# A hybrid attention and retention encoder layer: its prelude loaded in eight transfers on two queues, x scaled before it is turned, and larger loads in phase 1

## The chip, the cores and the metric

The kernel runs on one core of a Trainium2 chip. The metric is device time in microseconds (us) of one execution. Three runs of the kernel before took 971.65, 972.60 and 973.26 us, median 972.6 us.

## The reference, cut to what matters

x has 512 rows of 2048 columns, all f32. A vector `c` gives a shift and a scale for each column of x, and a gate for each column of the output:

```
c_act = silu(c)
shift, scale, gate = split(c_act @ w_ada + b_ada, 3)        # w_ada 2048 x 6144
h = x * rsqrt(mean(x*x over a row) + eps) * g * (1 + scale) + shift   # norm, then modulation
proj = h @ w_in                                             # 2048 x 7168
q, k, v, z of 8 attention heads and 4 retention heads = split(proj)
y = concat(attention(...) * silu(z_a), retention(...) * silu(z_r))
out = rms_norm(x + gate * (y @ w_out), final_gain)
```

(`g` multiplies the normed x before the modulation; the kernel puts it into the scale.) No product with `w_in` can start before some 128 columns of h are there, and these need the norm of whole rows of x, and `c_act @ w_ada` for those columns.

## The kernel before, in words

**Exact products from three passes.** Every large operand is split into a high part (float32r) and the rest. A product is three matmuls: high by high (line 85), and the two mixed ones (line 87). ScalarE writes the high part of a piece of w_in (`whi`, line 543), VectorE the rest (`wlo`, line 544). A matmul with 512 moving columns follows the one before it by 0.23 us when nothing is waited for.

**The columns of h are made tile by tile.** The 2048 columns are 16 "k-tiles" of 128. Phase 1 multiplies the first 13 units of `w_in` (256 columns each) with them in chunks of 1, 2, 2, 3, 4 and 4 k-tiles (`CHUNKS`), while the modulation of the next chunk is being made. One k-tile costs phase 1 78 matmuls of 512 moving columns (13 units, two 128-column halves or their like, three passes). Sums over chunks are kept in SBUF (`acc`, line 941, VectorE), except for two units that keep their PSUM banks.

**The modulation of a chunk** (`ada_pieces`, line 188): blocks of `w_ada` are loaded into `araw`, three buffers of 4 KB a partition; VectorE multiplies each by its entry of silu(c) and adds it to `aacc` (line 216; the first one is ScalarE's, line 212); TensorE sums over the partitions; then shift, scale, `hh` (high part, ScalarE, line 168) and `hl` (the rest, VectorE, line 181). The steps lie in an agenda that is spread over the items that are fed; a step adds the block loaded three steps earlier and then issues the next load.

**The feed** (`feed`): an item is half a load of `w_in` (512 columns' worth). It is loaded, four items later (`LEAD`) split, two items later (`LOOK`) multiplied. Loads of `w_in` go into `raw`, three buffers of 4 KB a partition.

**The prelude** makes all this possible. SyncE's queue issues everything in this order: eight loads of the first tile's columns of `w_ada` (line 110, 256 KB each, 512-byte runs), among them the small rows of `c`, `b_ada` and the gain (lines 115, 118, 119), then x in eight half tiles of 512 KB (line 127), then `w_in` and `w_ada` for phase 1. VectorE multiplies and adds the 16 blocks of `w_ada` (lines 279, 281); TensorE needs only four short products to sum them (`sums0`, line 288). For each of the four tiles of 128 rows of x, ScalarE makes the sums of squares of both halves (line 302), VectorE and GpSimd the row factor (lines 308, 315, 319). TensorE turns the unscaled x 128 columns at a time (`turned`, line 343), or turns and scales it by a product with a diagonal matrix (`turned_scaled`, `k0_part`, lines 351, 377); where it was turned unscaled, VectorE multiplies the result by factors that were spread over all partitions (lines 331, 335, 373). `WARM` products of constants (lines 392, 396) keep TensorE at work early on.

**What sets the order.** An engine executes its instructions in one order, which a scheduler chose and which pinned instructions (`pin`) fix. A transfer issued from SyncE or ScalarE is counted by one of eight completion semaphores, taken in turn by both queues together; the ninth transfer waits until the first has landed, and that wait stands in the issuing engine's own queue.

Of the kernel before, what the change touches and what calls it, by code (L numbers as in the profile page):

```python
# [17 lines left out]
P = 128  # L18
# [33 lines left out]
def trunk_kernel(ctx, tc, x, c, norm_gain, w_ada, b_ada, w_in, w_out, dec_f, dec_b, final_gain, out):  # L52
# [36 lines left out]
    # ---------------- loads of c, of the first tile's columns of w_ada, of x  # L89
# [4 lines left out]
    # x transposed lies where the low part of h comes to lie, a tile for each chunk of k  # L94
# [49 lines left out]
    nc.scalar.activation(ce, ps0[:, 0:NK], AF.Exp, scale=-1.0)
# [7 lines left out]
    # an engine keeps to the traced order of pinned instructions  # L152
# [11 lines left out]
    # ---------------- modulation of k-tiles k0..k0+nk, then their h  # L164
# [23 lines left out]
    def ada_pieces(k0, nk):  # L188
        n = nk * P
        acc = aap.tile([P, 2, 4 * P], F32, tag="aacc", name="aacc")  # L190
        npc = max(1, 1024 // (2 * n))
# [3 lines left out]
        def load(kr):  # L195
            raw = aap.tile([P, 1024], F32, tag="araw", name="araw", bufs=AR)
            rv = raw[:, : npc * 2 * n].rearrange("p (a b f) -> p a b f", a=npc, b=2)
            src = wa[kr * P : (kr + npc) * P, 0 : 2 * D].rearrange(
                "(a p) (b f) -> p a b f", p=P, b=2
            )[:, :, :, k0 * P : k0 * P + n]  # L200
            if npc == 1:
                nc.sync.dma_start(rv[:, 0], src[:, 0])
            else:
                for b in range(2):
                    nc.sync.dma_start(rv[:, :, b], src[:, :, b])
            raws[kr] = rv
# [66 lines left out]
    nc.vector.tensor_copy(bg, ps0[:, 64:112])
    nc.vector.tensor_scalar_add(bg[:, 16:32], bg[:, 16:32], 1.0)
    acc0 = [aap.tile([P, 2 * P], F32, tag="acc0", name="acc0") for _ in range(2)]
    for k in range(NK):
        rv, c1 = raw0[k // 4][:, k % 4], ct[:, k : k + 1]
        if k < 2:
            nc.vector.tensor_scalar_mul(acc0[k], rv, c1)
        else:  # L280
            nc.vector.scalar_tensor_tensor(acc0[k % 2], rv, c1, acc0[k % 2], op0=ALU.mult, op1=ALU.add)
    rsb = aap.tile([P, S], F32, name="rsb", bufs=1)

    def sums0():
        psa = bank(psA, "psa")
        for i in range(2):
            for b in range(2):
                nc.tensor.matmul(
                    psa[:, b : b + 1], acc0[i][:, b * P : (b + 1) * P], ones[:, 0:1],
                    start=i + b == 0, stop=i == 1, skip_group_check=True,  # L290
                )
        return psa

    def shift_scale0(psa):
        nc.vector.tensor_tensor(sv[:, 0:1], psa[:, 0:1], bg[:, 0:1], op=ALU.add)
        nc.vector.tensor_tensor(av[:, 0:1], psa[:, 1:2], bg[:, NK : NK + 1], op=ALU.add)
        nc.vector.tensor_tensor(av[:, 0:1], av[:, 0:1], bg[:, 32:33], op=ALU.mult)

    def squares(t, h):
        sq = xp.tile([P, 1024], F32, tag="sq", name="sq")  # L300
        v = xn[t][:, h * 1024 : (h + 1) * 1024]
        marks["sq"] = pin(nc.scalar.activation(sq, v, AF.Square, accum_out=ssx[:, t, h : h + 1]))

    mss = {}

    def half_root(t):
        ms = mss[t] = small.tile([P, 2], F32, tag="ms2", name="ms2", bufs=2)
        pin(nc.vector.tensor_scalar(ms[:, 0:1], ssx[:, t, 0:1], 1.0 / D, EPS, op0=ALU.mult, op1=ALU.add))

    def roots(t):  # L310
        if t not in mss:
            half_root(t)
        ms = mss[t]
        pin(
            nc.vector.scalar_tensor_tensor(
                ms[:, 1:2], ssx[:, t, 1:2], 1.0 / D, ms[:, 0:1], op0=ALU.mult, op1=ALU.add
            )
        )
        nc.gpsimd.tensor_tensor(rsx[:, t : t + 1], ms[:, 1:2], mhalf[:, 0:1], op=ALU.pow)

    # the rows' factors: on a diagonal, then on every partition
    dgs = {}
    psbs = {}

    def diagonal(t):
        dg = dgs[t] = xp.tile([P, P], F32, tag="dg", name="dg", bufs=2)
        marks["dg"] = pin(nc.vector.tensor_scalar_mul(dg, ident, rsx[:, t : t + 1]))

    def spread(t):
        psb = bank(psA, "psb")[:, 0:P]  # L330
        pin(nc.tensor.matmul(psb, ones, dgs[t], start=True, stop=True))
        psbs[t] = psb

    def spread_out(t):
        pin(nc.vector.tensor_copy(rsb[:, t * P : (t + 1) * P], psbs[t]))
# [3 lines left out]
    def turned(t, b):  # L339
# [6 lines left out]
    def turned_scaled(t, b):  # L346
        ps = psx[t, b] = bank(psP, "psx")
        for j in range(4):
            k = 4 * b + j
            pin(  # L350
                nc.tensor.matmul(
                    ps[:, j * P : (j + 1) * P], xn[t][:, k * P : (k + 1) * P], dgs[t], start=True, stop=True
                )
            )

    def pieces(b):
        for i, g in enumerate(groups):
            lo, hi = max(g[0], 4 * b), min(g[-1] + 1, 4 * b + 4)
            if i and lo < hi:
                yield i, g, lo, hi  # L360

    def evacuated(t, b):
        for i, g, lo, hi in pieces(b):
            dst = xt_tiles[i][:, lo - g[0] : hi - g[0], t * P : (t + 1) * P]
            src = psx[t, b][:, (lo - 4 * b) * P : (hi - 4 * b) * P].rearrange("p (k f) -> p k f", k=hi - lo)
            pin(nc.scalar.copy(dst, src))

    def scaled(t, b):
        rt = rsb[:, t * P : (t + 1) * P].rearrange("p (a f) -> p a f", a=1)
        for i, g, lo, hi in pieces(b):  # L370
            dst = xt_tiles[i][:, lo - g[0] : hi - g[0], t * P : (t + 1) * P]
            src = psx[t, b][:, (lo - 4 * b) * P : (hi - 4 * b) * P].rearrange("p (k f) -> p k f", k=hi - lo)
            pin(nc.vector.tensor_tensor(dst, src, rt.to_broadcast([P, hi - lo, P]), op=ALU.mult))

    def k0_part(t):
        o = psk3[:, 0:P] if t == 3 else psk[:, t * P : (t + 1) * P]
        pin(nc.tensor.matmul(o, xn[t][:, 0:P], dgs[t], start=True, stop=True))

# [3 lines left out]
    # the first tile's h, its columns in two parts  # L382
# [8 lines left out]
    for _ in range(WARM):  # L391
        pin(nc.tensor.matmul(ps0[:, 128:256], ones, ident, start=True, stop=True))
    turned(0, 0)
    turned(0, 1)
    for _ in range(WARM2):
        pin(nc.tensor.matmul(ps0[:, 128:256], ones, ident, start=True, stop=True))
# [910 lines left out]
```

## Time and profile before

| what | value |
|---|---|
| times of three runs | 971.65, 972.60, 973.26 us (median 972.6) |
| profiled execution: its span, first to last instruction | 971.6 us (1.0 us under the median; no other time is given for it) |
| TensorE busy | 941.5 us, 97% of the span |
| VectorE busy | 618.0 us, 64% |
| ScalarE busy | 376.5 us, 39% |
| GpSimd busy | 10.6 us, 1% |
| read from HBM | 136.36 MB |
| share of the 16 DMA engines taken by SyncE's queue | 43.4% |

How to read it: times in views are microseconds from the first instruction. In the views PE is TensorE (PEld its weight loads), DVE is VectorE, ACT is ScalarE, POOL is GpSimd, SP is SyncE; SPq or ACTq is the engine's sequencer, which issues transfers. "idle before us <-releaser" in a row of groups, or the bracket in a row of the timeline, is how long the engine stood idle before it and what ended that. A row of windows gives, for each stretch, its length, busy time of PE, PEld, DVE, ACT and POOL with the number of instructions, the granted clock of TensorE as a share, the busy share of the 16 DMA engines and GB/s. A matmul in the program can be two instructions in the trace (f32 operands), and consecutive matmuls overlap.

### The profile page before, as it was taken

What the parts mean: (1) busy time and instruction counts of PE and PEld (TensorE: products, weight loads), DVE (VectorE), ACT (ScalarE), POOL (GpSimd) and SP (SyncE); (2) the same over time, 40 slices, a digit from 0 to 9 for tenths busy, and PEclk for the clock granted to TensorE, in tenths of its full rate; (3) what the DMA queues carried; (4) which work ended last, traced back from release to release, by engine and by line L of the source; (5) the groups of instructions that cost most, each with busy time, mean ns of one, the idle gap of its engine ahead of it and who ended that gap; (6) DMA issues with size and microseconds to landing.
All of it is one profiled execution on the core that took longest, in us unless ns stands there. A gap on an engine that the chain in (4) does not pass through costs nothing.

```text
span 971.6 us, 14377 instructions
## 1 busy us (share of the span) xinstructions
PE 941.5 (97%) x5556; PEld 820.4 (84%) x5556; DVE 618.0 (64%) x1101; ACT 376.5 (39%) x732; POOL 10.6 (1%) x22
## 2 busy tenths in 40 slices
PE   5989898999999999999999999999999999999996
PEld 4877687788988888988998899988899988888896
DVE  5879978977968786664555556745534382535444
ACT  3824242525235555444343232422333372333321
POOL 0000000000000000000000000000000000000001
PEclk9989999999999999999999999999999999999999
DMA  9786878763552222212224525425322148233304
GB/s 316 232 260 209 270 250 290 266 202 99 183 179 84 65 66 66 65 45 88 84 69 161 186 66 184 143 88 198 126 63 90 57 159 283 86 128 134 109 1 173
DMA packets 109715, 141.49 MB, mean 146 GB/s; under 512 B 6024, under 2 KB 78408, under 8 KB 109648
## 3 DMA queue, kind: packets, MB, share of 16 engines
q1 hardware_dynamic: 108496, 138.49, 43.4%
q10 hardware_dynamic: 1152, 2.10, 0.6%
q8 instruction: 43, 0.70, 0.3%
q14 instruction: 24, 0.20, 0.1%
HBM read 136.36 MB, written 4.20 MB: 145 GB/s over the span
## 4 chain that ended last, share of the span: by engine, by line
PE 89%; DMA 5%; DVE 3%; issue 2%; SPq 1%; ACT 0%; POOLq 0%; POOL 0%; DVEq 0%; ACTq 0%
PE pp L87 26%; PE pw L87 14%; PE pp L85 13%; PE po L87 12%; PE pw L85 7%; PE po L85 6%; PE op L87 3%; PE sp L87 2%; DMA raw<-in_w_in_dram 2%; DMA araw<-in_w_ada_dram 2%; PE op L85 2%; PE tp L770 1%; DVE aacc L216 1%; PE sp L85 1%; DMA xt<-in_x_dram 1%
## 5 line engine op out<-in xcount | busy, mean ns | idle before, releaser
L543 ACT CAST whi<-raw 128x512 fp32r<-128x512 f32 (+1 forms) x289 | 174.9, 606 | 435.8 <-PE pp L87 204.9
L544 DVE TENSOR_TENSOR wlo<-raw,whi 128x512 fp32r<-128x512 f32 (+1 forms) x289 | 193.9, 672 | 209.6 <-ACT whi L543 205.3
L85 PE MATMUL pp<-whi,hh 128*128 128x256 f32 x576 | 162.4, 282 | 0.0
L87 PE MATMUL pp<-wlo,hh 128*128 128x256 f32 x576 | 161.9, 281 | 0.0
L87 PE MATMUL pp<-whi,hl 128*128 128x256 f32 x576 | 161.5, 280 | 0.0
L85 PEld LDWEIGHTS pp<-whi,hh 128*128 128x128 f32 x576 | 108.5, 188 | 2.5 <-ACT sc L839 1.7
L87 PEld LDWEIGHTS pp<-wlo,hh 128*128 128x128 f32 x576 | 108.5, 188 | 1.0 <-DVE wlo L544 0.2
L87 PEld LDWEIGHTS pp<-whi,hl 128*128 128x128 f32 x576 | 108.5, 188 | 0.0
L85 PE MATMUL pw<-hh,whi 128*128 128x512 f32 x256 | 102.5, 401 | 3.6 <-DVE acc L941 3.6
L85 PE MATMUL pp<-hh,whi 128*128 128x512 f32 x256 | 102.7, 403 | 3.3 <-ACT hh L168 2.9
L87 PE MATMUL pp<-hh,wlo 128*128 128x512 f32 x256 | 102.1, 399 | 0.0
L87 PE MATMUL pp<-hl,whi 128*128 128x512 f32 x256 | 101.6, 397 | 0.0
L87 PE MATMUL pw<-hh,wlo 128*128 128x512 f32 x256 | 101.3, 396 | 0.0
L87 PE MATMUL pw<-hl,whi 128*128 128x512 f32 x256 | 101.1, 395 | 0.1
L87 PE MATMUL po<-wlo,yh 128*128 128x512 f32 (+1 forms) x252 | 92.6, 367 | 0.0
L85 PE MATMUL po<-whi,yh 128*128 128x512 f32 (+1 forms) x252 | 92.5, 367 | 0.0
L87 PE MATMUL po<-whi,yl 128*128 128x512 f32 (+1 forms) x252 | 92.5, 367 | 0.0
L216 DVE SCALAR_TENSOR_TENSOR aacc<-araw,ct,aacc 128x512 f32<-128x512 f32 (+2 forms) x75 | 76.1, 1014 | 10.8 <-DMA araw<-in_w_ada_dram 10.3
L941 DVE TENSOR_TENSOR acc<-acc,pw 128x512 f32<-128x512 f32 x100 | 66.3, 682 | 7.8 <-PE pw L87 7.3
L991 DVE SCALAR_TENSOR_TENSOR gacc<-graw,ct,gacc 128x512 f32<-128x512 f32 x60 | 45.0, 750 | 38.3 <-DMA graw<-in_w_ada_dram 38.0
L85 PEld LDWEIGHTS pp<-hh,whi 128*128 128x128 f32 x256 | 48.8, 191 | 16.7 <-ACT hh L168 3.0
L85 PEld LDWEIGHTS pw<-hh,whi 128*128 128x128 f32 x256 | 48.1, 188 | 17.3 <-DVE acc L941 5.7
(232 smaller groups left out, 1555.3 us busy)
## 6 DMA issues: line engine op xcount, KB each, us to landing
raw<-in_w_in_dram SPq DMA_DIRECT2D x94, 512.0 KB, 3.5
araw<-in_w_ada_dram SPq DMA_DIRECT2D x32, 512.0 KB, 5.5
graw<-in_w_ada_dram SPq DMA_DIRECT2D x64, 256.0 KB, 2.9
raw<-in_w_out_dram SPq DMA_DIRECT2D x32, 512.0 KB, 3.5
araw<-in_w_ada_dram SPq DMA_DIRECT2D x40, 256.0 KB, 3.7
raw<-in_w_in_dram SPq DMA_DIRECT2D x16, 384.0 KB, 5.4
araw<-in_w_ada_dram SPq DMA_DIRECT2D x16, 384.0 KB, 3.7
xt<-in_x_dram SPq DMA_DIRECT2D x8, 512.0 KB, 8.6
```

Source lines behind the costliest of these rows:

```text
L85: nc.tensor.matmul(o, lh, rh, start=start, stop=False, skip_group_check=True)
L87: nc.tensor.matmul(o, a, b, start=False, stop=stop and b is (rl if swap else rh), skip_group_check=True)
L216: ins = nc.vector.scalar_tensor_tensor(acc[:, :, :n], rv[:, a], ct[:, kr + a : kr + a + 1], acc[:, :, :n], op0=ALU.mult, op1=ALU.add,)
L543: c1 = nc.scalar.copy(dh, src)
L544: c2 = nc.vector.tensor_tensor(dl, src, f32(dh), op=ALU.subtract)
L770: nc.tensor.transpose(tp_[:, j * P : (j + 1) * P], pt[:, j * P : (j + 1) * P], ident)
L941: nc.vector.tensor_tensor(accs[u][i], accs[u][i], ps[i], op=ALU.add)
L991: nc.vector.scalar_tensor_tensor(st["acc"], raw, ct[:, kr : kr + 1], st["acc"], op0=ALU.mult, op1=ALU.add)
```

## The change

**Loads of the prelude.** The first tile's columns of `w_ada` come in four loads of 512 KB on SyncE's queue (two column blocks, `raw00` and `raw01`, shown as raw_105 and raw_106, in two halves of eight row blocks each). x comes in four loads of 1 MB on ScalarE's queue, a whole tile each. The rows of `c`, `b_ada` and the gain are issued by GpSimd, ahead of its constants. All loads of chunk 0's `w_in` are issued before anything of phase 1 is fed.

**The first tile's modulation.** VectorE's 16 multiplications and additions are gone. TensorE sums directly over rows with `w_ada` as the stationary operand and a column of silu(c) as the moving one: 32 products of one column (`sums0`), in four groups of eight, placed between the tiles of x.

**x.** Of a tile's squares ScalarE sums the left half (`squares_a`), VectorE the right half (a product that sums, with 1/D and eps in it). The factor then scales x in place before it is turned, on VectorE, in a 128-column piece, an 896-column piece, and later the right half. All turning is by the identity; results are copied out of PSUM by ScalarE (banks 0, 1, 3) and VectorE (bank 2). The diagonal, the spread factors and the products with them are gone. Products of constants stand in four places (`WARM = 8, 6, 5, 6`).

**Phase 1.** `araw` has 8 KB a partition, so that a step carries twice the row blocks of `w_ada`. Through the first four chunks every second load of `w_in` goes to one of three further buffers (`raw1`), and items are split eight items after they are loaded (`LEAD1`), from the fifth chunk on four as before. The last tile's results are copied out in four agenda steps from item 10 on.

```
-WARM = 9
-WARM2 = 1
-LATE_AT = 7, 8
+WARM = 8, 6, 5, 6
-RAW, WB, LOOK, LEAD, EB, YB = 3, 3, 2, 4, 1, 22
+RAW, RAW1, WB, LOOK, LEAD, LEAD1, EB, YB = 3, 3, 3, 2, 4, 8, 1, 22
...
     def raw_tile():
+        early["n"] += 1
+        if early["on"] and early["n"] % 2 == 0:
+            return aap.tile([P, 1024], F32, tag="raw1", name="raw1", bufs=RAW1)
         return wp.tile([P, 1024], F32, tag="raw", name="raw", bufs=RAW)
...
+    def load0(q, b, i):
+        q.dma_start(
+            raw0[b][:, i * 8 : (i + 1) * 8],
+            wa[i * 8 * P : (i + 1) * 8 * P, b * D : b * D + P].rearrange("(a p) f -> p a f", p=P),
+        )
+
+    for t in range(NT):
+        nc.scalar.dma_start(xn[t], x2[t * P : (t + 1) * P, :])
+    nc.gpsimd.dma_start(c_row, c.rearrange("b (k p) -> (b k) p", p=P))
+    for i in range(2):
+        for b in range(2):
+            load0(nc.sync, b, i)
+    nc.gpsimd.dma_start(bg_row[0:32, :], b_ada[:, 0 : 2 * D].rearrange("b (k p) -> (b k) p", p=P))
+    nc.gpsimd.dma_start(bg_row[32:48, :], norm_gain.rearrange("b (k p) -> (b k) p", p=P))
...
-        npc = max(1, 1024 // (2 * n))
+        npc = 2048 // (2 * n)
...
-            raw = aap.tile([P, 1024], F32, tag="araw", name="araw", bufs=AR)
+            raw = aap.tile([P, 2048], F32, tag="araw", name="araw", bufs=AR)
...
+    def sums0(b, i):
+        for a in range(8 * i, 8 * i + 8):
+            pin(
                 nc.tensor.matmul(
+                    psa[:, b : b + 1], raw0[b][:, a, :], ct[:, a : a + 1],
+                    start=a + b == 0, stop=a == NK - 1, skip_group_check=True,
                 )
+            )
...
+    warm(WARM[0])
+    squares_a(0)
+    squares(0)
+    silu_c()
+    for t in range(NT):
+        scaled(t, 0, P)
+        k0_part(t)
+        if t == 3:
+            break
+        scaled(t, P, 1024)
+        turned(t, 0)
+        turned(t, 1)
+        squares_a(t + 1)
+        squares(t + 1)
+        if t < 2:
+            warm(WARM[1 + t])
         if t == 0:
+            turn_rows()
+        else:
+            sums0(t - 1, 0)
+        evacuated(t, 0, act)
+        evacuated(t, 1, act)
+    for t in range(3):
+        scaled(t, 1024, D)
+        turned(t, 2)
+        turned(t, 3)
+        evacuated(t, 3, act)
+        if t:
+            evacuated(t - 1, 2, dve)
+    sums0(0, 1)
+    scaled(3, P, 1024)
+    evacuated(2, 2, dve)
+    marks["conv1"] = [marks[act], marks[dve]]
+    sums0(1, 1)
+    warm(WARM[3])
+    shift_scale0()
...
+        lead = LEAD1 if early["on"] else LEAD
+        while len(loaded) > (lead if item is not None else 0):
...
+        early["on"] = ci < len(CHUNKS) - 2
...
+        if ci == 0:
+            for it in items:
+                it["load"]()
```

ScalarE at the start of the program, before (sq is the junk result of the squares, xt_122 and xt_125 the first two tiles of x, psx a PSUM bank with turned x, DMAHW a completion semaphore of a transfer):

```order
L144 ACT_TABLE_LOAD
L144 ACTIVATE ce<-ps_145 128x16 [waits PE_49]
L302 ACTIVATE sq,ssx<-xt_122 128x1024 [waits DMAHW3_49]
L302 ACTIVATE sq,ssx<-xt_122 128x1024 [waits DMAHW4_49,Activation_49]
L302 ACTIVATE sq,ssx<-xt_125 128x1024 [waits DMAHW5_49,Activation_49]
L302 ACTIVATE sq,ssx<-xt_125 128x1024 [waits DMAHW6_49,Activation_49]
L366 COPY xT_96<-psx 128x4x128 [waits PE_49]
```

ScalarE at the start of the program, now (xt_107 to xt_110 are the four tiles of x):

```order
L121 DMA xt_107<-in_x_dram 128x2048
L121 DMA xt_108<-in_x_dram 128x2048
L121 DMA xt_109<-in_x_dram 128x2048
L121 DMA xt_110<-in_x_dram 128x2048 [waits DMAHW2_49]
L300 ACT_TABLE_LOAD
L300 ACTIVATE sqa,ssx<-xt_107 128x1024 [waits DMAHW0_49]
L272 ACTIVATE ce<-ps_143 128x16 [waits PE_49]
L300 ACTIVATE sqa,ssx<-xt_108 128x1024 [waits DMAHW3_49]
```

The four loads of x now stand ahead of all that ScalarE computes, and the fourth waits for semaphore 2; the rows after it, the table load and the first squares, stand behind that wait.

TensorE where the first tile's modulation is summed, before (acc_160 and acc_161 are VectorE's sums, dg the diagonal of row factors):

```order
L288 MATMUL psa<-ones,acc_160 128x1 [waits DVE_49]
L288 MATMUL psa<-ones,acc_160 128x1
L288 MATMUL psa<-ones,acc_161 128x1 [waits DVE_49]
L331 MATMUL psb<-dg,ones 128x128 [waits DVE_49]
L377 MATMUL psk<-dg,xt_122 128x128
L351 MATMUL psx<-dg,xt_122 128x128 x4
```

TensorE in the same part, now (raw_105 and raw_106 are the two column blocks of w_ada):

```order
L353 MATMUL ps_143<-ident,ones 128x128 x5
L286 MATMUL psa<-ct,raw_105 128x1 [waits DMAHW1_49]
L286 MATMUL psa<-ct,raw_105 128x1 x7
L322 MATMUL psk<-ident,xt_109 128x128 [waits DMAHW6_49,DVE_49]
L328 MATMUL psx<-ident,xt_109 128x128 [waits DVE_49,PE_49,Activation_49]
L328 MATMUL psx<-ident,xt_109 128x128 x2
L286 MATMUL psa<-ct,raw_106 128x1 [waits DMAHW2_49]
L286 MATMUL psa<-ct,raw_106 128x1 x7
L322 MATMUL psk_144<-ident,xt_110 128x128 [waits DMAHW2_49,DVE_49]
```

Four short products became 32, eight of them between two tiles of x, and the rows name semaphore 2 as that of SyncE's second load, the first half of raw_106.

TensorE just ahead of the first product with w_in, before:

```order
L351 MATMUL psx<-dg,xt_128 128x128 x8
L343 MATMUL psx<-ident,xt_131 128x128 x3
L377 MATMUL psk_307<-dg,xt_131 128x128
L343 MATMUL psx<-ident,xt_131 128x128 x4
L331 MATMUL psb<-dg,ones 128x128
L85 MATMUL pw<-hh_77,whi 128x512
```

TensorE just ahead of the first product with w_in, now:

```order
L328 MATMUL psx<-ident,xt_107 128x128 x8
L328 MATMUL psx<-ident,xt_108 128x128 x8
L328 MATMUL psx<-ident,xt_109 128x128 x8
L286 MATMUL psa<-ct,raw_105 128x1 x8
L286 MATMUL psa<-ct,raw_106 128x1 x8
L353 MATMUL ps_143<-ident,ones 128x128 x6
L328 MATMUL psx<-ident,xt_110 128x128 x7
L89 MATMUL pw<-hh_77,whi 128x512
```

The right halves of three tiles, half of the short products, six products of constants and seven turns of the last tile now stand in a row ahead of the first product.

More of the change, by code (lines that the diff above doesn't have):

```diff
@@ L200, in load @@
             )[:, :, :, k0 * P : k0 * P + n]
[L201 to L205, printed above, removed]
+            for b in range(2):
+                nc.sync.dma_start(rv[:, :, b], src[:, :, b])
             raws[kr] = rv
@@ L267, in ada_pieces @@
         )
-    nc.tensor.transpose(ps0[:, 64:112], bg_row, ident[0:48, 0:48])
     bg = const.tile([P, 48], F32, name="bg")
[L273 to L287, printed above, removed]
+    def turn_rows():
+        pin(nc.tensor.transpose(ps0[:, 64:112], bg_row, ident[0:48, 0:48]))
+        pin(nc.vector.tensor_copy(bg, ps0[:, 64:112]))
+        pin(nc.vector.tensor_scalar_add(bg[:, 16:32], bg[:, 16:32], 1.0))
+    def silu_c():
+        pin(nc.tensor.transpose(ps0[:, 0:NK], c_row, ident[0:NK, 0:NK]))
+        pin(nc.scalar.activation(ce, ps0[:, 0:NK], AF.Exp, scale=-1.0))
+        pin(nc.vector.tensor_scalar_add(ce, ce, 1.0))
+        pin(nc.vector.reciprocal(ce, ce))
+        pin(nc.vector.tensor_tensor(ct, ps0[:, 0:NK], ce, op=ALU.mult))
@@ L288, in sums0 @@
+    psa = bank(psA, "psa")
+    psk = bank(psA, "psk")
+    ps0 = bank(psA, "ps0")
+    psk3 = bank(psM, "psk3")
+    def sums0(b, i):
+        for a in range(8 * i, 8 * i + 8):
+            pin(
                 nc.tensor.matmul(
-                    psa[:, b : b + 1], acc0[i][:, b * P : (b + 1) * P], ones[:, 0:1],
-                    start=i + b == 0, stop=i == 1, skip_group_check=True,
-                )
[L292 to L297, printed above, removed]
@@ L314, in roots, with squares @@
+    def squares(t):
+        sd = aap.tile([P, 1024], F32, tag="aacc", name="sqd")
+        v = xn[t][:, 1024:2048]
+        pin(nc.vector.tensor_tensor_reduce(sd, v, v, 1.0 / D, EPS, ALU.mult, ALU.add, ssx[:, t, 1:2]))
+        ms = small.tile([P, 1], F32, tag="ms1", name="ms1", bufs=2)
         pin(
             nc.vector.scalar_tensor_tensor(
-                ms[:, 1:2], ssx[:, t, 1:2], 1.0 / D, ms[:, 0:1], op0=ALU.mult, op1=ALU.add
+                ms, ssx[:, t, 0:1], 1.0 / D, ssx[:, t, 1:2], op0=ALU.mult, op1=ALU.add
@@ L317, in roots @@
             )
         )
[L319 to L335, printed above, removed]
+        nc.gpsimd.tensor_tensor(rsx[:, t : t + 1], ms, mhalf[:, 0:1], op=ALU.pow)
@@ L337, in trunk_kernel, with scaled, k0_part, turned @@
+    def scaled(t, a, b):
+        v = xn[t][:, a:b]
+        marks["sc"] = pin(nc.vector.tensor_scalar_mul(v, v, rsx[:, t : t + 1]))
     psx = {}
-    def turned(t, b):
+    def k0_part(t):
+        o = psk3[:, 0:P] if t == 3 else psk[:, t * P : (t + 1) * P]
+        pin(nc.tensor.transpose(o, xn[t][:, 0:P], ident))
+    def turned(t, b, pin=pin):
         ps = psx[t, b] = bank(psP, "psx")
@@ L343, in turned, with evacuated @@
             pin(nc.tensor.transpose(ps[:, j * P : (j + 1) * P], xn[t][:, k * P : (k + 1) * P], ident))
[L346 to L356, printed above, removed]
+    def evacuated(t, b, eng):
         for i, g in enumerate(groups):
@@ L359, in pieces @@
             if i and lo < hi:
[L360 to L377, printed above, removed]
+                dst = xt_tiles[i][:, lo - g[0] : hi - g[0], t * P : (t + 1) * P]
+                src = psx[t, b][:, (lo - 4 * b) * P : (hi - 4 * b) * P].rearrange("p (k f) -> p k f", k=hi - lo)
+                marks[eng] = pin(eng(dst, src))
+    act, dve = nc.scalar.copy, nc.vector.tensor_copy
     hl[0] = hp.tile([P, 1, S], F32R, tag="g0", name="hl0")[:, 0, :]
@@ L389, in h0_low @@
         marks["hl"] = pin(nc.vector.tensor_tensor(hl[0][:, cols], tmp0[:, cols], f32(hh[0][:, cols]), op=ALU.subtract))
[L391 to L396, printed above, removed]
-    turned(0, 3)
-    for t in range(2):
-        squares(t, 0)
-        squares(t, 1)
-    roots(0)
-    psa = sums0()
@@ L403, in trunk_kernel @@
-    psk = bank(psA, "psk")
-    diagonal(0)
-    shift_scale0(psa)
-    spread(0)
-    k0_part(0)
-    spread_out(0)
-    for t in range(2):
-        turned_scaled(t, 2)
-        evacuated(t, 2)
-        squares(t + 2, 0)
-        squares(t + 2, 1)
-        scaled(t, 0)
-        turned(t + 1, 0)
-        half_root(t + 1)
-        scaled(t, 1)
-        turned(t + 1, 1)
-        roots(t + 1)
-        scaled(t, 3)
-        if t == 0:
-            turned(1, 3)
-        diagonal(t + 1)
-        if t == 1:
-            half_root(3)
-        spread(t + 1)
-        k0_part(t + 1)
-        spread_out(t + 1)
@@ L429, in trunk_kernel, with warm @@
-    marks["conv1"] = [marks["sq"]]
-    psk3 = bank(psM, "psk3")
-    turned_scaled(2, 2)
-    turned_scaled(2, 3)
-    roots(3)
-    scaled(2, 0)
-    turned(3, 0)
-    diagonal(3)
-    marks["conv1"].append(marks["dg"])
-    k0_part(3)
+    def warm(n):
+        for _ in range(n):
+            pin(nc.tensor.matmul(ps0[:, 128:256], ones, ident, start=True, stop=True))
+    warm(WARM[0])
[14 more added lines that the diff above has]
+            warm(WARM[1 + t])
+        if t == 0:
+            turn_rows()
[3 more added lines that the diff above has]
+        evacuated(t, 1, act)
@@ L446, in trunk_kernel @@
     h0_low(B)
-    spread(3)
-    turned(3, 2)
-    evacuated(2, 3)
-    turned(3, 3)
-    spread_out(3)
-    scaled(3, 0)
-    scaled(3, 1)
-    late = [lambda b=b: scaled(3, b) for b in (2, 3)]
+    scaled(3, 1024, D)
+    for b in range(4):
+        turned(3, b, lambda ins: ins)
+    late = [lambda b=b: evacuated(3, b, act if b % 2 else dve) for b in range(4)]
     x_scope.close()
@@ L889, in trunk_kernel @@
     fed = 0
-    for i, f in zip(LATE_AT, late):
-        agenda.setdefault(i, []).append(f)
+    for i, f in enumerate(late):
+        agenda.setdefault(LEAD1 + LOOK + i, []).append(f)
     def plan(fs, start, span):
```

59 lines of the change are left out of this document (15 added, 44 removed).

## The prediction

> **What bounds the kernel now.** I read the page's busy line, then windows, then the waits of the engine that fills them.
>
> ```profile
> span 971.6 us, 14377 instructions
> PE 941.5 (97%) x5556; PEld 820.4 (84%) x5556; DVE 618.0 (64%) x1101; ACT 376.5 (39%) x732; POOL 10.6 (1%) x22
> ```
>
> TensorE is the bound; only its 30 idle us and its slow clock can be won. The first product with w_in, then the windows after it:
>
> ```profile
> 28.75 0.50 PE L85 MATMUL pw<-hh,whi 128*128 128x512 f32 x1
> ```
>
> ```profile
> 28.00:40.00 12.00, 11.91 (x58) 9.18 (x58) 11.99 (x26) 10.62 (x22) 0.00 (x0) 1.00 0.58 181
> 40.00:50.00 10.00, 9.60 (x64) 8.39 (x62) 8.29 (x14) 6.21 (x13) 0.00 (x0) 1.00 0.87 272
> 50.00:60.00 10.00, 7.05 (x23) 5.71 (x23) 5.46 (x11) 2.98 (x5) 0.00 (x0) 0.66 0.82 259
> 60.00:110.00 50.00, 49.99 (x251) 41.52 (x250) 48.00 (x74) 16.95 (x34) 0.00 (x0) 1.00 0.73 235
> 110.00:170.00 60.00, 53.33 (x314) 45.33 (x313) 49.97 (x69) 19.62 (x42) 0.00 (x0) 1.00 0.80 272
> 170.00:220.00 50.00, 50.00 (x222) 39.92 (x223) 42.03 (x61) 20.30 (x53) 0.00 (x0) 1.00 0.69 228
> ```
>
> So the prelude costs 28.75 us, and phase 1 loses TensorE time at two places. In 50 to 60, 2.95 us are idle and the granted clock is 0.66: 10 x 0.34 = 3.4 us lost. In 110 to 170, 6.67 us are idle. With 0.5 ahead of 50 the losses are 13.5 us. After 170 TensorE has no gap, so a later first product carries to the end one for one. The waits behind the two places (the first row PE's from 28 to 240 us, the second VectorE's from 28 to 200: total, how often, longest), and the timeline at the first:
>
> ```profile
> PE pw L85 <- DVE acc L941: 4.7, 6, 1.7
> ```
>
> ```profile
> DVE aacc L216 <- DMA araw<-in_w_ada_dram: 8.7, 11, 3.2
> ```
>
> ```profile
> 49.18 1.05 PE L230 MATMUL psm<-ones,aacc 128*128 128x1 f32 x8 [0.40 <-DVE aacc L216]
> ...
> 51.80 0.62 ACT L543 CAST whi<-raw 128x512 fp32r<-128x512 f32 x1 [3.42 <-DMA raw<-in_w_in_dram]
> 52.32 1.51 ACT L168 ACTIVATE hh<-xT,sv,av 128x512 fp32r<-128x512 f32 x2
> 53.18 2.07 PE L85 MATMUL pp<-hh,whi 128*128 128x512 f32 x4 [2.95 <-ACT hh L168]
> ```
>
> At 50, `hh` of chunk 1 stood behind a split on ScalarE that waited for w_in. At 110 to 170, VectorE waits in its order for w_ada, so `acc` comes late and TensorE waits for a bank.
>
> **Terms won in phase 1.** Now chunk 0's w_in is all issued first and splits follow loads by eight items, so I take the 3.42 us wait away; what is late next at the boundary is VectorE. Its rows:
>
> ```profile
> L216 DVE SCALAR_TENSOR_TENSOR aacc<-araw,ct,aacc 128x512 f32<-128x512 f32 x18 | 13.4, 747 | 0.9 <-DMA araw<-in_w_ada_dram 0.8
> L544 DVE TENSOR_TENSOR wlo<-raw,whi 128x512 fp32r<-128x512 f32 x7 | 4.8, 687 | 2.0 <-ACT whi L543 1.8 <-DMA raw<-in_w_in_dram 0.2
> L544 DVE TENSOR_TENSOR wlo<-raw,whi 128x256 fp32r<-128x256 f32 x5 | 2.1, 420 | 0.6 <-ACT whi L543 0.6
> ```
>
> Chunk 1 needs 16 blocks x 0.75 = 12.0, splits 4 x 0.69 + 5 x 0.42 = 4.9, and some 3.3 for h and copies: 20.2 us, begun about 1.6 before the first product. Chunk 0 keeps TensorE from 28.75 to about 48.8, 20.0 us. So h is ready about when TensorE is (18.6 against 20.0): I count the 0.5 + 2.95 and the 3.4 of slow clock as won, 6.8.
>
> In 110 to 170 VectorE is busy 49.97 and waits 8.7, together nearly all of 60. A step now brings 1 MB, and three steps' lead is therefore twice the data ahead. If no wait is left, TensorE wins 6.7; if the larger load merely lands as much later, nothing. The row 60 to 110, VectorE busy 48.0 of 50 and TensorE without a gap, says that VectorE keeps up when its data are there; but it has no slack for a late block. I leave 2.5 of the 6.7. **Won: 6.8 + 6.7 - 2.5 = 11.0** (ends 6.8, and 15 with the refill after each stall).
>
> **Terms of the prelude.** The transfers:
>
> ```profile
> 0.00:2.00 2.00, 0.00 (x0) 0.00 (x0) 0.07 (x1) 1.27 (x1) 0.93 (x9) 1.00 0.02 7
> 8.00:12.00 4.00, 3.68 (x19) 3.42 (x18) 3.89 (x12) 0.00 (x0) 0.00 (x0) 1.00 1.02 293
> 16.00:20.00 4.00, 2.97 (x18) 2.89 (x18) 2.64 (x13) 2.56 (x6) 0.68 (x2) 0.75 1.03 416
> 22.00:24.00 2.00, 1.98 (x17) 1.60 (x15) 1.56 (x7) 1.38 (x3) 0.00 (x0) 1.00 1.07 360
> 26.00:28.00 2.00, 2.00 (x20) 2.00 (x20) 1.29 (x5) 1.96 (x5) 0.55 (x1) 1.00 0.82 283
> ```
>
> W_ada in 512-byte runs came at 293 GB/s, x at 416, with the engines full in both; nothing comes in the first 2 us. Two queues move no more bytes than one that fills the engines; they only change who is first.
>
> *The wait that is added.* x's fourth load, on ScalarE, waits for SyncE's second load. Behind it in ScalarE's queue stand the table load, the first squares and silu(c), and behind these everything. Before, no compute stood behind an issue there. When does that load land (A)? If bytes are shared evenly, 1.05 MB of w_ada and as much x are through: 3.6 + 2.5 + 2.0 = 8.1. If three tiles of x go first: 3.15 / 0.416 = 7.6, + 3.6 + 2.0 = 13.2. No row shows two load queues sharing, so I take the middle, 10.7. From there, rows of the first 60 us, then of the whole span:
>
> ```profile
> L302 ACT ACTIVATE sq<-xt 128x1024 f32<-128x1024 f32 x8 | 8.5, 1059 | 9.8 <-DMA xt<-in_x_dram 9.5
> L302 ACT ACTIVATION_READ_ACCUMULATOR sq<-xt 128x1 f32 x8 | 1.5, 188 | 0.0
> L144 ACT ACT_TABLE_LOAD x1 | 1.3, 1283 | 0.7 <-PEq L1296 0.7
> L319 POOL TENSOR_TENSOR rsx<-ms,mhalf 128x1 f32<-128x1 f32 x4 | 2.2, 553 | 23.5 <-DVE ms L315 23.5
> L327 DVE TENSOR_SCALAR dg<-ident,rsx 128x128 f32<-128x128 f32 x4 | 1.1, 287 | 0.7 <-POOL rsx L319 0.4
> L373 DVE TENSOR_TENSOR xT<-psx,rsb 128x512 f32<-128x512 f32 x4 | 2.7, 684 | 0.0
> L288 PE MATMUL psa<-ones,acc 128*128 128x1 f32 x8 | 0.9, 240 | 0.0
> ```
>
> ```profile
> L755 DVE CUSTOM_DVE_ANT_0 pt<-sp,ad 128x512 f32<-128x512 f32 x32 | 21.0, 685 | 0.5 <-PE sp L87 0.5
> L755 DVE DVE_READ_ACCUMULATOR2_ANT nm<- 128x1 f32 x32 | 2.7, 83 | 0.0
> L1199 DVE CUSTOM_DVE_ANT_0 otmp<-res 128x256 f32<-128x256 f32 x4 | 1.7, 425 | 0.1
> L1219 DVE TENSOR_SCALAR res<-res,rsf 128x512 f32<-128x512 f32 x12 | 5.1, 482 | 1.9 <-POOL rsf L1210 1.9
> ```
>
> ScalarE: 0.5 to issue, table 1.28, square 1.06, reading 0.19: T0 = A + 3.0. VectorE then chains the tiles. A right half's squares: 425 ns at 256 and 685 at 512 columns make 1.21 at 1024, with the reading 1.29. Scaling: 287 ns at 128, 482 at 512 make 0.68 at 896 and 0.74 at 1024. A root (VectorE, GpSimd 0.55, two handovers): 0.9. So tile 0: 0.9 + 0.29 + 0.68 = 1.87; tile 1: 1.29 + 1.87 + 0.8 (an estimate: VectorE waits for the turned rows of b_ada behind eight turns) = 3.96; tile 2: 3.16; tile 3's first piece 2.48; three right halves and tile 3's second piece 3 x 0.74 + 0.68 = 2.9. T0 + 14.4. TensorE's earlier turns and ScalarE's copies lie beside this. Then TensorE alone, at 0.11 to 0.12 per instruction (17 in 1.98, 20 in 2.00): eight turns 0.9, 16 short products of two instructions each 3.8 (32 x 0.12), six constant products 1.3, seven turns 0.8: 6.8; shift, scale and `hh` end beside the last two. First product by this chain: A + 3.0 + 14.4 + 6.8 = A + 24.2 = 34.9 (32.3 to 37.4).
>
> *The other limit* is x's last tile: x 4.2 MB and chunk 0's w_in 1.7 at 416, w_ada 2.1 at 293: 14.2 + 7.2 + 2.0 = 23.4 (19.3 without w_in ahead), then 1.29 + 0.9 + 0.29 + 2.9 + 6.8 = 12.2: 35.6. I take the later, 35.6.
>
> *Clock.* TensorE, idle through the hold and half idle between tiles, had 0.75 in 16 to 20 us under such work and 1.00 in 22 to 28. I charge half speed for 3.4 us, which is 1.7 lost; ends 0 and 6.8. First product: **37.3, that is 8.6 later.**
>
> The removed VectorE additions and the diagonal save nothing by themselves: the new chain ends later. The rows of c, b_ada and the gain on GpSimd's queue cost nothing under the hold; without it, ScalarE's exponential would wait for c, at worst until data come at all, some 2 us in. The last tile's copies, moved behind the first product, are in VectorE's 3.3 above; ScalarE, busy 10.62 of 12 there, has 1.4 to spare.
>
> **A rule against the even sharing.** In the middle I let w_ada get some of the engines beside x. The Trainium skill, "DMA: Bandwidth & Descriptors", section "Queues, rings and completion order", says that a DMA engine takes queues in turn packet by packet; x's 8 KB runs would then crowd out w_ada's 512-byte ones. By it A is 13.2, the first product 39.1, the time 972.0; no run here shows it yet.
>
> **Sum.** 971.6 - 11.0 + 8.6 = 969.2 for the profiled execution; that stands 1.0 under the median, so **970.2**. The measurement tells 0.2% from no change: faster is under 970.65, slower over 974.55.
>
> **Rivals.**
>
> 1. *Slower: the closing products at half clock.* Everything that TensorE does alone ahead of the first product (6.8 us) doubles, + 5.1 over the forecast: 975.3; if tile 1's share (eight turns, five constants, eight short products, 3.9 us against VectorE's 3.16) is slow too, about 977. I take 976.3. It decides from + 4.4, a closing part over 12.9 us. For it: 0.75 in 16 to 20, 0.66 after a 2.95 gap. Against: 1.00 from 22 to 28, and the constants put in. The Trainium skill, "TensorE: Matmul & The Clock Gate", Part 4 on PE-mode transpose, says that transposes do not count as busy for the clock gate; by it this rival would hold. Before's row of 22 to 28, at 1.00, mixes both kinds and does not settle it.
> 2. *The hold is short.* W_ada gets its share, x's last tile lands by 22: first product 34.0 (between 32.3 and 35.6), 5.2 later: 971.6 - 11.0 + 5.2 + 1.0 = 966.8. For it: the engines carry both sizes at over 290 GB/s. Against: the 8 KB runs.
> 3. *All of phase 1's stalls go*, refills too: 971.6 - 15 + 8.6 + 1.0 = 966.2. For it: VectorE had 8.7 us of waits to give. Against: 48.0 of 50 busy in 60 to 110.
> 4. *The larger loads bring nothing* from 110 on: 6.8 won, 974.4; it is the forecast's own upper end.
>
> **Chances.** Forecast 0.42, own range 967.5 to 974.4 (faster 0.20, same 0.20, slower 0.02). Half clock 0.24 (slower 0.20, same 0.04). Short hold 0.14 and all stalls gone 0.14, both faster. The rest 0.06: both of these together, 962.8 (faster 0.03); or the boundary at chunk 1 stalls again with its slow clock, 6.4 more, 976.6 (slower 0.03). Faster 0.51, same 0.24, slower 0.25. Leaving out the 962.8 below and what of the slow clock lies above, the range is 963.5 to 977.0.
>
> **What would show it.** ScalarE's first square begins 2 us or so behind the end of SyncE's second load, near 12.5 us, though x's first tile landed before; if it begins at the landing of x, the added wait is wrong. The first product at 37.3 (over 40: clock; under 35: short hold). Granted clock of the last 9 us ahead of it: near 0.8; under 0.6 is rival 1. No gap over 1 us and clock 1.00 in the ten us after chunk 0. VectorE's waits for w_ada after 100 us under 4 in place of 8.7. A gain with a first product before 30 us would make the whole prelude part wrong.

## The result: slower by 1%

| | before | now |
|---|---|---|
| times, median | 972.12 us (4 runs, 970.59 to 973.26) | 981.54 us (4 runs, 980.36 to 985.70) |
| ratio, 95% interval | | 1.0105 (1.0078 to 1.0132) |
| span of the profiled execution | 971.6 us | 979.1 us |
| first product with w_in | 28.75 us | 44.77 us |

The forecast was a small gain, 970.2, with a range that ended at 977.0; the kernel became slower and lies outside it. The first product is 16.0 us later, not 8.6. Phase 1 gives back 8.5 of these (16.0 less the 7.5 between the spans), not 11.0.

The changed kernel's page, and the timeline at the first product:

```profile
span 979.1 us, 14412 instructions
PE 949.8 (97%) x5614; PEld 828.9 (85%) x5614; DVE 615.6 (63%) x1079; ACT 374.5 (38%) x738; POOL 12.3 (1%) x25
```

```profile
44.77 0.48 PE L89 MATMUL pw<-hh,whi 128*128 128x512 f32 x1
```

TensorE's share looks as good as before; the busy line does not tell that some of its busy time is at half speed. The chain of waits that ended last in the first 46 us, in order of time (start, us, what), shows where the time went:

```profile
1.24 13.37 DMA raw<-in_w_ada_dram
...
14.63 0.34 ACTq L121
...
15.00 1.28 ACT L300
...
16.29 1.16 ACT sqa L300 x2
...
19.32 1.76 PE psx L328 x7
21.08 2.56 PE ps L353 x12
...
27.31 1.68 PE psa L286 x16
...
29.92 2.47 PE psa L286 x16
...
32.71 4.99 PE psx L328 x24
37.70 3.64 PE psa L286 x32
41.35 2.77 PE ps L353 x12
44.12 0.90 PE psx L328 x7
```

Up to 15 us everything hangs on SyncE's second load, issued at 1.24 us (line 121 is x's fourth load, which waits for it on ScalarE). From 29 us on the chain is TensorE's alone: sums (line 286), turns (328), constants (353). Equal work takes unequal time in it: 16 instructions of the sums 1.68 us, then 2.47. Windows of 3.4 us, with the granted clock third from the end:

```profile
27.30:30.70 3.40, 3.40 (x34) 3.40 (x33) 2.63 (x7) 1.72 (x6) 0.55 (x1) 0.99 1.09 348
30.70:34.10 3.40, 3.40 (x18) 3.40 (x18) 1.58 (x3) 0.00 (x0) 0.00 (x0) 0.50 0.83 262
34.10:37.50 3.40, 3.40 (x18) 3.40 (x17) 2.63 (x5) 1.17 (x2) 0.00 (x0) 0.51 0.01 3
37.50:40.90 3.40, 3.40 (x33) 3.40 (x31) 0.20 (x1) 1.10 (x2) 0.00 (x0) 0.99 0.00 0
40.90:44.40 3.50, 3.50 (x18) 3.50 (x18) 2.85 (x9) 2.44 (x5) 0.00 (x0) 0.52 0.20 63
```

TensorE is busy without a gap in all five, and half as many instructions pass in three of them. And phase 1, where it answers to the rows of before:

```profile
50.00:60.00 10.00, 9.92 (x50) 7.93 (x49) 7.67 (x14) 9.86 (x23) 0.00 (x0) 1.00 0.85 271
60.00:110.00 50.00, 49.66 (x262) 40.78 (x261) 48.56 (x79) 20.00 (x39) 0.00 (x0) 1.00 0.85 281
110.00:170.00 60.00, 57.33 (x336) 48.65 (x335) 55.04 (x78) 23.34 (x59) 0.00 (x0) 1.00 0.85 293
```

The stall at the boundary to chunk 1 with its slow clock is gone, and of the 6.67 idle us from 110 to 170, 2.67 are left.

### The profile page after: what moved, and what is told of

Same layout as the page of the kernel before. It is cut to its first block, busy times and chain, and to the rows that moved or that the text cites. A ratio compares the mean times of both kernels' runs of the same rounds, so it can differ in the third digit from the quotient of the medians.

```text
span 979.1 us, 14412 instructions
## 1 busy us (share of the span) xinstructions
PE 949.8 (97%) x5614; PEld 828.9 (85%) x5614; DVE 615.6 (63%) x1079; ACT 374.5 (38%) x738; POOL 12.3 (1%) x25
## 4 chain that ended last, share of the span: by engine, by line
PE 90%; DMA 4%; DVE 3%; issue 1%; ACT 1%; POOL 0%; SPq 0%; POOLq 0%; DVEq 0%; ACTq 0%
PE pp L91 24%; PE pw L91 15%; PE pp L89 12%; PE po L91 12%; PE pw L89 8%; PE po L89 6%; PE op L91 3%; PE sp L91 2%; DMA graw<-in_w_ada_dram 2%; PE op L89 2%; PE tp L721 1%; DMA raw<-in_w_ada_dram 1%; PE sp L89 1%; PE psx L328 1%; PE psa L286 1%
## 5 line engine op out<-in xcount | busy, mean ns | idle before, releaser
L89 PEld LDWEIGHTS pw<-hh,whi 128*128 128x128 f32 x256 | 48.1, 188 | 17.8 <-DVE acc L893 4.5
```

Source lines behind the costliest of these rows:

```text
L89: nc.tensor.matmul(o, lh, rh, start=start, stop=False, skip_group_check=True)
```

## The experiments

All ratios are to the kernel before, timed on the same chip. The runs used more than one chip; by its median the kernel before took 971.1 to 972.2 us on them, so times of different runs are compared to about 1 us.

**1. x's last tile off ScalarE's queue.**

```diff
-    for t in range(NT):
+    for t in range(NT - 1):
         nc.scalar.dma_start(xn[t], x2[t * P : (t + 1) * P, :])
...
             load0(nc.sync, b, i)
+    nc.sync.dma_start(xn[3], x2[3 * P : 4 * P, :])
```

> x's last tile is issued on SyncE's queue behind w_ada, so nothing of ScalarE's stands behind a transfer's landing. Theory H (the wait for SyncE's second load is what made it slower): the first square starts at about 7.5 us instead of 16.3, the first product with w_in comes at 33 to 35 us instead of 44.8, then set by the landing of x's last tile; time about 971. Theory C (TensorE's half clock ahead of the first product is the cost, wherever the hold ends): the first square is early too, but the stretches of half clock stay and the first product is at 38 or later; time 975 or more.

Measured: 974.30 us, 1.0028 (1.0015 to 1.0041). ScalarE's first square, the first product, and the windows ahead of it:

```profile
7.14 1.06 ACT L301 ACTIVATE sqa<-xt 128x1024 f32<-128x1024 f32 x1 [3.37 <-DMA xt<-in_x_dram]
```

```profile
37.10 0.48 PE L89 MATMUL pw<-hh,whi 128*128 128x512 f32 x1
```

```profile
8.00:24.00 16.00, 11.39 (x80) 10.41 (x80) 8.67 (x25) 7.08 (x21) 2.21 (x4) 0.98 1.09 361
24.00:37.00 13.00, 12.73 (x75) 12.63 (x75) 7.55 (x17) 4.73 (x9) 0.00 (x0) 0.63 0.86 272
```

The square starts 9.15 us earlier, the first product 7.7. So moving this one load wins 7.7 us at the first product and about 7 of the time (981.5 less 974.3). It is not the whole price of the hold, because another limit took over: SyncE comes to x's last tile only at 13.14 us, behind the loads of w_ada, and its squares wait for it until 21.2:

```profile
13.14 1.74 SPq L126 DMA_DIRECT2D xt<-in_x_dram  x1
```

```profile
21.21 1.06 ACT L301 ACTIVATE sqa<-xt 128x1024 f32<-128x1024 f32 x1 [4.05 <-DMA xt<-in_x_dram]
```

The result, 37.1 us and 974.3, lies between the two theories. Theory H is right on the hold; theory C is right on what is left: the clock is 0.63 in the last 13 us.

**2. Both kinds of loads in one queue**, w_ada first:

```diff
-    for t in range(NT):
-        nc.scalar.dma_start(xn[t], x2[t * P : (t + 1) * P, :])
...
             load0(nc.sync, b, i)
+    for t in range(NT):
+        nc.sync.dma_start(xn[t], x2[t * P : (t + 1) * P, :])
```

> The changed kernel with x's four loads on SyncE's queue behind the four of w_ada, none on ScalarE's. If x's long runs in the other queue were what kept w_ada's second load until 15 us: that load lands at 5.5 to 6.5, x's first tile at 11 to 12, its last at 19 to 20, and no stretch of ScalarE waits for w_ada. First product 12 + 25.5 = 37 with its stretches of half clock, 971.5 + 0.4 + 1.8 = 974. If w_ada is as slow alone: it lands after 10, and the first product comes after 41.

Measured: 977.58 us, 1.0066 (1.0041 to 1.0092). The issues of the first 30 us (KB each, median us to landing), in the changed kernel and here:

```profile
xt<-in_x_dram ACTq DMA_DIRECT2D x4, 1024.0 KB, 8.3
...
raw<-in_w_ada_dram SPq DMA_DIRECT2D x4, 512.0 KB, 12.1
```

```profile
raw<-in_w_ada_dram SPq DMA_DIRECT2D x4, 512.0 KB, 6.0
```

```profile
12.78 1.06 ACT L300 ACTIVATE sqa<-xt 128x1024 f32<-128x1024 f32 x1 [10.76 <-DMA xt<-in_x_dram]
```

```profile
41.40 0.48 PE L89 MATMUL pw<-hh,whi 128*128 128x512 f32 x1
```

W_ada's loads take 6.0 us alone and 12.1 beside x's. So they are not slow by themselves, they are crowded out. First product and time are 3.4 and 4.0 us earlier than in the changed kernel; at 41.4 the first product is 4.4 later than I expected, because what follows the first square takes as long as there (28.6 against 28.5 us), with its half clock.

**3. TensorE at work through the hold.**

```diff
-WARM = 8, 6, 5, 6
+WARM = 46, 6, 5, 6
```

> 46 products of constants instead of 8 ahead of the first tile, so that TensorE is at work through the hold. Theory C: granted clock 1.00 instead of 0.50 from 16 to 24 us, the wait for the turned rows (3.3 us) shrinks, and the first product comes 3 us earlier or more; time about 978. Theory H alone: the first product moves by under 1 us; time 981. If the later half clock (31 to 37 and 41 to 44 us) depends on the early one, it goes too and the time is 975.

Measured: 980.05 us, 1.0095 (1.0070 to 1.0121): not told apart from the changed kernel. First product at 43.39, and three stretches ahead of it:

```profile
16.00:24.00 8.00, 5.36 (x30) 4.70 (x28) 3.02 (x10) 5.24 (x12) 1.11 (x2) 0.79 1.06 378
24.00:36.00 12.00, 11.01 (x97) 10.62 (x98) 9.24 (x20) 5.50 (x14) 1.09 (x2) 1.00 0.86 275
36.00:43.40 7.40, 7.40 (x40) 7.40 (x39) 3.72 (x10) 2.44 (x5) 0.00 (x0) 0.54 0.11 35
```

1.4 us of the 3 expected. The constants ended at 16.9 us, and TensorE stood idle for the 2.18 us ahead of the first turn, at 19.20; the half clock came there too (0.79 from 16 to 24), so the early stretch was shortened and not removed. The half clock near the end comes all the same: the idle hold is not its cause.

From 24 to 36 us the clock is 1.00, although the first two groups of sums, 16 instructions each, stand there. In the changed kernel the clock halved behind the second of them. So such a group does not cost half clock each time; in every profile of this form of the sums it came during or behind the last 32 in a row.

**4. The short products exchanged for constant products**, in number and place.

```diff
-        for a in range(8 * i, 8 * i + 8):
+        warm(7)
+        for a in ((0,), (15,))[i]:
```

> Of the 32 one-column products that sum the first tile's modulation, 28 are replaced by products of constants with 128 moving columns (the sums leave out 28 of 32 row blocks); the number of TensorE instructions and their places stay. Theory O (a window full of one-column products is followed by half clock): granted clock 1.00 from 24 us to the first product, which comes about 5 us earlier, at 39.7; time about 976.5. Theory T (turning by transposes does not count as work for the clock): the half clock stays from 31 to 37 us, where 24 turns stand, and the first product moves by under 2 us; time 980 or more.

Measured: 976.84 us, 1.0062 (1.0044 to 1.0079).

```profile
16.00:24.00 8.00, 4.55 (x21) 4.02 (x21) 3.06 (x10) 5.11 (x12) 1.11 (x2) 1.00 1.06 381
24.00:40.00 16.00, 15.07 (x133) 14.67 (x134) 10.98 (x25) 6.91 (x17) 1.10 (x2) 1.00 0.69 219
```

```profile
16.64 1.06 ACT L301 ACTIVATE sqa<-xt 128x1024 f32<-128x1024 f32 x1
...
19.66 1.75 PE L329 MATMUL psx<-ident,xt 128*128 128x128 f32 x7
...
24.44 0.33 PE L323 MATMUL psk<-ident,xt 128*128 128x128 f32 x1 [0.69 <-DVE xt L317]
25.03 0.98 PE L329 MATMUL psx<-ident,xt 128*128 128x128 f32 x7 [0.27 <-DVE xt L317]
...
40.06 0.48 PE L89 MATMUL pw<-hh,whi 128*128 128x512 f32 x1
```

In the changed kernel the second tile's first turn stood here:

```profile
24.61 0.33 PE L322 MATMUL psk<-ident,xt 128*128 128x128 f32 x1 [0.70 <-DVE xt L316]
```

From first square to first product 23.4 us instead of 28.5, 5.1 us less, with the 31 turns still there. Theory O holds, theory T falls. Nothing was changed ahead of 26 us, and up to the second tile's first turn 0.5 of the 5.1 are won (7.80 us from the first square instead of 8.32); behind it, where the products were exchanged, 4.5.

The clock column misleads ahead of its first change: it says 1.00 from 16 to 24, but seven turns took 1.75 us, as in the changed kernel at 0.50 (1.76), and 0.98 for the next tile. So the early half clock is there in this run too, and ended a little sooner.

**5. The same sums with w_ada moving**, upon experiment 1.

```diff
-                    psa[:, b : b + 1], raw0[b][:, a, :], ct[:, a : a + 1],
+                    psa[0:1, P + b * P : 2 * P + b * P], ct[:, a : a + 1], raw0[b][:, a, :],
...
+    def turn_sums():
+        row = const.tile([1, 2 * P], F32, name="row")
+        pin(nc.vector.tensor_copy(row, psa[0:1, P : 3 * P]))
+        warm(WARM[3])
+        for b in range(2):
+            pin(
+                nc.tensor.matmul(
+                    psa[:, b : b + 1], row[:, b * P : (b + 1) * P], ones[0:1, 0:1],
```

> x's last tile on SyncE's queue as in the first run, and the sums with the operands changed over: a column of silu(c) stands, 128 columns of w_ada move, the row that comes out is copied (VectorE) and turned by two products of one row. As many TensorE instructions as before, and two more. Theory O in the form that the number of moving columns in a window sets the clock: 1.00 from 24 us on, first product 37.1 - 5.1 + 0.8 = 32.8 us, time about 970. In the form that the part of the array at work sets it (here one column of 128): the half clock stays and the first product is at 37 to 38.5; time 974 to 976.

Measured: 972.64 us, 1.0006 (0.9990 to 1.0021): the loss is gone.

```profile
24.00:35.00 11.00, 9.74 (x80) 7.87 (x79) 6.07 (x13) 3.31 (x7) 0.00 (x0) 1.00 1.00 320
```

```profile
35.04 0.49 PE L89 MATMUL pw<-hh,whi 128*128 128x512 f32 x1 [0.65 <-ACT hh L358]
```

The clock is 1.00 although one column of the array holds weights: in these two runs it is the moving columns that count. The first product is 2.1 us earlier than in run 1, not 4.3: VectorE waits 1.8 for the row and 1.7 for its turn.

**6. The changed prelude with the phase 1 of before** (all edits of phase 1 undone):

> The changed prelude with the phase 1 of before (512 KB a step of w_ada, three buffers, splits four items after their loads, no loads ahead). If the 8.5 us won behind the first product belong to the larger and earlier loads: first product near 44.8 and the time 979.1 + 8.5 + 2.4 (median over the profiled run) = 990. If they belong to the late first product, which gives VectorE and the loads time: time 982 to 984.

Measured: 986.86 us (984.59 to 995.35), 1.0166 (1.0108 to 1.0224). In between: of the 8.5 us, 5 or so are the new phase 1's; that the others come with the later first product is what remains, not shown by a trace. The intervals of this and the changed kernel overlap, so the shares are rough. Its profiled execution is its longest; nothing is read from it.

**7. The prelude of before with the phase 1 of now** (all edits of phase 1 made; the last tile's copies stand at agenda steps 11 and 12 instead of 7 and 8, in runs 9 and 10 too):

> The prelude of before with the phase 1 of after (loads of 1 MB a step, three more buffers, splits eight items after their loads, chunk 0's loads all first). If the two parts are independent: first product at 28.8 us, and the 8.5 us that phase 1 won in the changed kernel stay: 963.6. Rival: these were won because the late prelude left VectorE time ahead of the first product; then the stall at the boundary to chunk 1 comes back, with its slow clock, and the time is 967 to 970.

Measured: 968.25 us, 0.9971 (0.9959 to 0.9983). The first product is at 26.93, earlier than in the profile of before with the same prelude: from 18 to 20 us the clock was 0.5 there and is 1.00 here, and in runs 8 to 10 (first product 26.9 to 27.4). So some 1 us or more of what separates these profiles from that of before lies in its prelude, not in phase 1. What set that clock was not found out. Then:

```profile
46.78 1.05 PE L232 MATMUL psm<-ones,aacc 128*128 128x1 f32 x8 [0.78 <-DVE aacc L218]
49.19 1.65 PE L90 MATMUL pp<-hh,whi 128*128 128x512 f32 x3 [1.36 <-ACT hh L173]
```

```profile
45.00:50.00 5.00, 2.86 (x15) 2.15 (x14) 4.31 (x10) 2.30 (x4) 0.00 (x0) 0.83 1.09 353
49.00:56.00 7.00, 6.81 (x18) 5.38 (x19) 4.99 (x8) 2.13 (x5) 0.00 (x0) 0.56 0.80 258
```

The rival holds: the boundary stalls for 2.1 us, first on VectorE's sums and then on the `hh` that follows from them, and the slow clock comes back.

**8. Only the steps of 1 MB**, in the kernel before:

```diff
...
-        npc = max(1, 1024 // (2 * n))
+        npc = 2048 // (2 * n)
...
-            raw = aap.tile([P, 1024], F32, tag="araw", name="araw", bufs=AR)
+            raw = aap.tile([P, 2048], F32, tag="araw", name="araw", bufs=AR)
```

> The kernel before, with only the steps of w_ada in phase 1 doubled to 1 MB. If VectorE's waits for w_ada are what cost 6.7 us from 110 to 170: most of these go, the stall at the boundary to chunk 1 stays (ScalarE's split waits for w_in): 965 to 967. Rival, the larger load only lands later: 971.

Measured: 963.87 us, 0.9912 (0.9878 to 0.9946), more than expected and the lowest median of all: it beats both kernels. VectorE's waits from 26 to 200 us, and TensorE from 110 on:

```profile
DVE aacc L216 <- DMA araw<-in_w_ada_dram: 2.7, 4, 1.1
```

```profile
110.00:170.00 60.00, 59.01 (x343) 50.62 (x342) 55.81 (x78) 27.14 (x62) 0.00 (x0) 1.00 0.90 301
```

The waits for w_ada fall from 8.7 to 2.7 us and the idle time from 6.67 to 0.99. The boundary still stalls (TensorE busy 3.24 of 5 us from 45 to 50), but without half clock in this profile. That, and the earlier first product (27.36), may be what it wins over the expectation.

**9. Only the three buffers, the earlier splits and chunk 0's loads ahead**, in the kernel before:

> The kernel before, with only the three further buffers, the splits eight items after their loads and chunk 0's loads first. If ScalarE's split in its order behind a late load of w_in is the whole cause of the stall at 50 us: it goes, 6 us less, 965. If VectorE is as late there (run with the prelude of before: h at 49.2 against TensorE's 46.8): the stall shrinks to 1 to 3 us, its slow clock stays, and the waits of 110 to 170 stay: 969 to 971.

Measured: 977.84 us, 1.0049 (1.0031 to 1.0067): slower, against both expectations. VectorE's waits from 26 to 200 us, and TensorE at the boundary:

```profile
DVE aacc L221 <- DMA araw<-in_w_ada_dram: 12.5, 14, 2.6
```

```profile
48.35 1.05 PE L235 MATMUL psm<-ones,aacc 128*128 128x1 f32 x8 [2.32 <-DVE aacc L221]
```

The waits rise from 8.7 to 12.5, and TensorE waits 2.32 us for VectorE's sums at the boundary, where it was 0.40. That this comes from w_in's loads, which now stand ahead of w_ada's in one queue, is argued from the order of issues; no run separates the three edits.

**10. As 7, but splits four items after their loads.**

```diff
-RAW, RAW1, WB, LOOK, LEAD, LEAD1, EB, YB = 3, 3, 3, 2, 4, 8, 1, 22
+RAW, RAW1, WB, LOOK, LEAD, LEAD1, EB, YB = 3, 3, 3, 2, 4, 4, 1, 22
```

> The prelude of before, steps of 1 MB, the three further buffers and chunk 0's loads first, but splits four items after their loads, as before. If the longer way from load to split is what costs (loads of w_in stand ahead of w_ada in SyncE's queue): near 964. If the further buffers or chunk 0's loads ahead cost: 967 to 969, as with the whole of phase 1.

Measured: 967.53 us, 0.9959 (0.9937 to 0.9981): its median is near run 7's, which speaks for the further buffers or chunk 0's loads ahead as what costs, and against the longer way; but its interval overlaps that of run 8, and this is not settled.

**11. The changed kernel with only the steps of 1 MB in phase 1:**

> The changed kernel without its three further buffers, earlier splits and chunk 0's loads ahead; its prelude and the steps of 1 MB stay. If the earlier loads take from phase 1 what the larger ones give, as with the prelude of before (968.3 with both, 963.9 with the larger loads alone): 977 to 978 against 981.5. If they cost only where the first product is early: no change, 981 to 982.

Measured: 983.37 us, 1.0119 (1.0095 to 1.0144): not told apart from the changed kernel. Behind a late first product no cost of the early loads can be told; behind the early one they, with the later copies of the last tile, took 4 to 6 us (runs 7 and 8: 4.4 by the medians, 5.7 by the ratios).

## Why the prediction was wrong, by its steps

- **What failed in the prelude** are two sizes of the sum: the landing of SyncE's second load, and the time lost to the clock. The added wait itself was named rightly; the first square begins 1.7 us behind that landing, as it said.
- **The landing was put in the middle of its two ends, 10.7.** It came at 14.6, 3.9 us later. Even the upper end, 13.2, was low. The step had no row for two queues that share, and took a middle where the upper end was nearer. The Trainium skill, "DMA: Bandwidth & Descriptors", section "Queues, rings and completion order", has engines take queues in turn by packets; by it x comes first, and the 12.1 against 6.0 us of run 2 agree. From the landing to the end of the first square's reading ScalarE took 2.8 us instead of 3.0.
- **The clock was charged with 1.7 us.** Run 4 measures 5.1 in all, 4.5 of it from the one-column products, which the sum priced by their number alone. That is 3.4 more than charged. Rival 1 put the loss in the right stretch, but it let all of it run at half speed (5.1 more), and its suspected cause, the turns, was wrong; over the last 9 us the clock was about 0.7, between the forecast's sign (0.8) and the rival's (under 0.6). In the changed kernel, 34.1 to 37.5 us hold turns alone, and the next window has the clock back (0.99). "TensorE: Matmul & The Clock Gate" in the Trainium skill, Part 4, says that the full clock does not engage for PE-mode transposes, which do not count as busy in the same way. If the turns here are such transposes, which no view names, these rows do not agree.
- **The limit by x's last tile (35.6)** did not act: the chain behind the hold did, 0.7 us less in the sum.
- **The chain behind the first row sum** came out near its size: 14.4 + 6.8 = 21.2, and without the late half clock (run 4, from 17.8, behind its square and reading, to 40.06) 22.3. That is partly luck. VectorE's wait for the turned rows of b_ada was estimated at 0.8 and took 2.8 in run 4: six products of constants, which the estimate left out, stand ahead of that turn, and part of them ran at half speed.
- Together 37.3 + 3.9 - 0.2 + 3.4 - 0.7 + 1.1 = 44.8; measured 44.8.
- **Phase 1: 11.0 forecast, 8.5 won.** Both places changed as forecast, and 2.67 idle us were left where I left 2.5; that the two agree is partly luck, since part of the win seems to come with the late start (run 6). By the windows 28 to 170, now with 0.72 idle between 45 and 50, 9.7 are won, 1.2 more than the 8.5. Of these, some 0.4 are a slip: the 3.4 us of slow clock were counted over 0.8 us in which TensorE was idle as well. Another 0.5 are idle time from 600 to 800 us (199.43 busy of 200 now, 199.97 before). The step failed in what it credited: the early loads win nothing that can be told (runs 9 and 11), the larger ones do (run 8). The term "ScalarE's split in the way" was half the truth: with it gone, VectorE was late (run 7), which I had judged at 18.6 against 20.0 us.
- **The median over the profiled run** was taken as 1.0 us; here it is 2.4.
- 970.2 + 7.4 + 2.5 + 1.4 = 981.5. The sum closes by its making, because the 8.5 us of phase 1 are what the spans leave.

## What to carry to other kernels

A transfer that waits for another one's landing holds all that stands behind it on the issuing engine; if a queue of long runs shares the engines with one of short runs, price that landing with the long runs first. Many products of one moving column can look like a full TensorE and halve its clock; let the long operand move. And try the parts of a combined change alone: here four lines, the larger steps, were 0.9% faster by themselves, and the rest more than undid it.

## What the runs showed of the hardware

- The profile's busy share of TensorE is not what the clock goes by: in the changed kernel 3.40 us busy of 3.40, with some 2.5 us of one-column products, were followed by 0.50. The same two groups of products passed at 1.00 in run 3.
- The granted clock of the views reads 1.00 until its first change in the record, and need not be so. In run 3 constants passed at 6 or 7 a microsecond from 4 to 9 us and at 11 from 10 to 16, all under 1.00. Compare the instructions' own durations.
- While w_ada's 512-byte runs moved alone, the engines were full at some 290 GB/s; while x's loads were in flight beside them, 405 moved in the changed kernel:

```profile
8.00:10.00 2.00, 0.00 (x0) 0.00 (x0) 0.00 (x0) 0.00 (x0) 0.00 (x0) 1.00 1.03 405
...
12.00:14.00 2.00, 0.00 (x0) 0.00 (x0) 0.00 (x0) 0.00 (x0) 0.00 (x0) 0.50 1.21 291
```

- After stalls of about two microseconds at the boundary to chunk 1 the clock halved in run 7 (0.56 from 49 to 56) and not in run 8. Which stall does it was not found out.
